# Rotary tables in three parts, a new order of the first lists, and one sum of squares, in a two-layer hybrid encoder

## The chip, the cores and the metric

The kernel runs on one core of one Trainium2 chip. The core has a matrix engine (TensorE, "PE" in the profile; its weight loads appear as "PEld"), a vector engine (VectorE, "DVE"), a scalar engine (ScalarE, "ACT"), a general engine (GpSimd, "POOL"), and a queue engine (SyncE, "SP") that issues the transfers of this kernel. The metric is device time in microseconds (us) for one execution. Each time is one of several runs, of which the median is given.

## The reference, cut to what matters

The input is one sequence of 2048 positions with 1024 features. Two layers are applied, then a final RMS norm. Each layer projects the normed rows to eight sections of 512 columns: query, key, value and gate of an attention with 8 heads of 64, and the same four for a retention with 4 heads of 128.

```python
def rotary_tables(positions, dim):
    inv_freq = 1.0 / (ROPE_BASE ** jnp.linspace(0.0, 1.0, dim // 2, dtype=jnp.float32))
    ang = positions.astype(jnp.float32)[:, None] * inv_freq[None, :]
    return jnp.cos(ang), jnp.sin(ang)

def apply_rotary(t, cos, sin):
    t1, t2 = jnp.split(t, 2, axis=-1)
    ...
    return jnp.concatenate([t1 * c - t2 * s, t1 * s + t2 * c], axis=-1)

def hybrid_layer(x, norm_gain, w_in, w_out, rel_bias, cos, sin):
    hn = rms_norm(x, norm_gain)
    proj = hn @ w_in.astype(hn.dtype)
    aq, ak, av, ag, rq, rk, rv, rg = jnp.split(proj, cuts, axis=-1)
    ya = chunked_rel_attention(aq..., ak..., av..., rel_bias)     # own chunk of 64 + 8 chunks before, softmax
    yr = chunkwise_retention(rq..., rk..., rv..., cos, sin)       # running state per head, rotary phases, group norm
    y = jnp.concatenate([ya * silu(ag), yr * silu(rg)], axis=-1)
    return x + y @ w_out.astype(x.dtype)
```

The kernel needs, for each of the 2048 positions, a table of 64 cosines and one of 64 sines. They are the same for all heads and both layers.

## The kernel before, in words

**Tiling.** The sequence is cut into 16 tiles of 128 rows ("tokens" t = 0 to 15 in the names) and 4 supertiles (n) of 512. The heads are cut into 4 groups (s), each of two attention heads and one retention head. A block is one (layer l, group s, supertile n); there are 32 of them. Single precision is made from pairs of half-precision parts, high and low (`hTh`, `hTl` for the normed and transposed rows, `whT`, `wlT`, `whV`, `wlV` for the weights), with three products for each pair.

**One block.** `dense_T` (line 637) makes the queries and keys in transposed form (tile `dT`, matmuls at line 763). In it, `tab_load` (lines 642 to 647) loads two tables for the supertile, `tabc` (cosine) and `tabs` (sine with its sign), each 128 partitions by 512 columns. The retention's queries and keys are turned in three GpSimd products (lines 703 to 705): the raw rows times `tabc`, the rows with swapped halves (`swp`, two transfers at lines 699 and 700) times `tabs`, and their sum. `dense_V` (line 770) makes values and gates (`dV`, matmuls at line 783). Attention of the block before runs between these matmuls: scores S (lines 831 and 832), bias and maximum on VectorE (line 835), exponent on ScalarE, a scaling on GpSimd (`pq`, line 841), a transpose by a transfer (`pT`, line 843, on SP), and the product with the values (lines 853 and 854).

**The tables.** `tables(ns, wk)` (line 83) computes the angles, the cosine (`k2`), the sine (`r`) and its negative (`ang`) for one or two supertiles in 18 steps. In the work tiles the 128 partitions hold two halves of 64 frequencies: the first 64 partitions for the first 256 positions of the supertile, the other 64 for the second 256. Positions are loaded, spread over 64 partitions, for each half by itself (line 90). `store` (lines 123 to 132) writes the tables to device memory, `tab_d[n]`, with two parts of 128 rows: cosine twice, then negative sine and sine. The supertiles 0; 1 and 2; 3 are computed by three such generators, called in the lists as the steps `t`, `u` and `v`.

**What sets the order.** On TensorE, VectorE, ScalarE and GpSimd the order of instructions is that of the program. In the startup, until the first supertile's `dV` is done, SP's order is that of the program too (`sp_order`, line 1313, left at line 1527). Later a scheduler orders SP's queue, except for transfers marked `in_turn`. The startup's order is written out by hand: one list of step names in `do(...)` (line 1449), in which `x..` steps belong to tokens (`sq` square, `rs` inverse root, `mul` scaling, `tr`, `hi`, `lo` the pair, `dma` the transposes, by transfer, of tokens 4 and up), `W` and `V` steps to weight sections, `g` to gains, `d` to the first block's dense work, `r` to the retention's constants, `bs` and `bt` to the bias. A second list, `listed` (line 1454), gives for each round of the following blocks what is done before and behind the attention step of the round; `run` takes one pair from it per round. Rounds 0 to 11 are `dV` of supertile 0, 12 to 35 the block of supertile 1, 36 to 59 that of supertile 2, 60 to 83 that of supertile 3.

**The output weights.** Before the output projection, `prep_Omax` (line 505) adds up the squares of all output weights of a layer, for one scale: eight slices of 128 columns are loaded (`stO0m`, `stO1m`), squared on ScalarE with the sum of each partition, and added on VectorE slice by slice (lines 520 and 522); then the partitions are summed by a matmul with ones.

Of the kernel before, what the change touches and what calls it, by code (L numbers as in the profile page):

```python
# [10 lines left out]
F32 = mybir.dt.float32  # L11
I32 = mybir.dt.int32
AF = mybir.ActivationFunctionType
ALU = mybir.AluOpType
AX = mybir.AxisListType
# [3 lines left out]
P = 128  # L19
# [8 lines left out]
def hybrid_trunk(ctx: ExitStack, tc: tile.TileContext, x, pos, gain, gcol, w_in, w_out, rel, fgain,  # L28
# [4 lines left out]
    KT = D // P  # L33
    NT = SEQ // P
    NS = SEQ // 512
    NSW = 4
    act, dve, pool, pe, sp = nc.scalar, nc.vector, nc.gpsimd, nc.tensor, nc.sync
# [29 lines left out]

    y_d = [dp.tile([P, D], F32, tag=f"y_d{t}", name=f"y_d{t}") for t in range(NT)]
    x_d = [dp.tile([P, D], F32, tag=f"x_d{t}", name=f"x_d{t}") for t in range(NT)]
    tab_d = [dp.tile([2, P, 512], F32, tag=f"tab{n}", name=f"tab{n}") for n in range(NS)]  # L70


    TWO_PI = 6.283185307179586
# [9 lines left out]
    def tables(ns, wk):  # L83

        ang, k, r, k2 = wk
        pi = k2.bitcast(I32)
        for i, n in enumerate(ns):
            for hf in range(2):
                o = n * 512 + hf * 256
                sp.dma_start(pi[hf * 64:(hf + 1) * 64, i * 256:(i + 1) * 256], pos[None, o:o + 256].to_broadcast([64, 256]))  # L90
        yield

        def mulsub(dst, kk, c):
            dve.scalar_tensor_tensor(out=dst, in0=kk, scalar=-c, in1=dst, op0=ALU.mult, op1=ALU.add)

        def rnd(dst, src, mul):
            dve.tensor_scalar(dst, src, mul, MAGIC, op0=ALU.mult, op1=ALU.add)
            dve.tensor_scalar(dst, dst, -MAGIC, None, op0=ALU.add)  # L98

        act.activation(ang, pi, AF.Copy, scale=invf_sb[:, 0:1])  # L100
        yield
        rnd(k, ang, 1.0 / P1)
        yield
        for c in (PA, PB, PC):
            mulsub(ang, k, c)
            yield
        dve.scalar_tensor_tensor(out=k2, in0=k, scalar=-(PD + PE_), in1=ang, op0=ALU.mult, op1=ALU.add)
        yield
        rnd(k2, k2, 1.0 / TWO_PI)
        yield  # L110
        for kk, c in ((k2, QA), (k, PD), (k2, QB), (k, PE_), (k2, QC)):
            mulsub(ang, kk, c)
            yield
        dve.tensor_scalar(ang, ang, PI_CL, -PI_CL, op0=ALU.min, op1=ALU.max)
        yield
        dve.scalar_tensor_tensor(out=k, in0=ang, scalar=-1.0, in1=ang, op0=ALU.mult, op1=ALU.max)
        yield
        act.activation(r, ang, AF.Sin)
        act.activation(k2, k, AF.Sin, scale=-1.0, bias=quarter[:, 0:1])
        yield  # L120
        act.activation(ang, r, AF.Copy, scale=-1.0)
        yield
        def store(i, n, hf):
            sl = slice(hf * 64, hf * 64 + 64)
            cs = slice(hf * 256, hf * 256 + 256)
            ws = slice(i * 256, i * 256 + 256)
            sp.dma_start(tab_d[n][0, 0:64, cs], k2[sl, ws])
            sp.dma_start(tab_d[n][0, 64:128, cs], k2[sl, ws])
            sp.dma_start(tab_d[n][1, 0:64, cs], ang[sl, ws])
            sp.dma_start(tab_d[n][1, 64:128, cs], r[sl, ws])  # L130
            if hf == 1:
                tab_done.add(n)

        for hf in range(2):
            store(0, ns[0], hf)
            if len(ns) > 1:
                later(7 + 4 * hf, lambda hf=hf: store(1, ns[1], hf))
        yield

    TAB_STEPS = 18  # L140
# [175 lines left out]
    def sumsq(sts, nm, dst):  # L316

        m1 = b2.tile([P, len(sts)], F32, tag="m1", name=f"m1{nm}", bufs=4)
        for i, (st, k0, k1) in enumerate(sts):
            act.activation(st if dst is None else dst[:, k0:k1, :], st, AF.Square, accum_out=m1[:, i:i + 1])  # L320
        if len(sts) == 2:
            dve.tensor_tensor(m1[:, 0:1], m1[:, 0:1], m1[:, 1:2], op=ALU.add)
        return m1[:, 0:1]

    def lowp(m1, nm):
        mb = b2.tile([P, 1], BF16, tag="mb", name=f"mb{nm}", bufs=4)
        dve.tensor_copy(mb, m1)
        return mb
# [175 lines left out]

    def prep_Omax(l, go):
        nm = f"O{l}"
        mm = b2.tile([P, 1], F32, tag="omax", name=f"omax{nm}")
        load = lambda j: load_sec(w_out[l, :, j * P:(j + 1) * P], f"{nm}m{j}")
        for _ in range(4):
            yield  # L510
        sts = [load(0), load(1)]
        for _ in range(4):
            yield
        for j in range(KT):
            yield
            m1 = sumsq(sts[j], f"{nm}m{j}", None)
            if j + 2 < KT:
                sts.append(load(j + 2))
            if j == 0:
                dve.tensor_copy(mm, m1)  # L520
            else:
                dve.tensor_scalar(mm, mm, 1.0, m1[:, 0:1], op0=ALU.mult, op1=ALU.add)
        mm = lowp(mm, nm)
        for _ in range(5):
            yield
        m = allsum(mm, nm)
        sv, iv = norm_scale(m, nm)
        go.os = b2.tile([P, 1], F32, tag="o_s", name=f"o_s{l}")
        go.oi = b2.tile([P, 1], F32, tag="o_i", name=f"o_i{l}")
        dve.tensor_copy(go.os, sv)  # L530
        dve.tensor_copy(go.oi, iv)
        yield
# [73 lines left out]
    def in_turn(i):  # L606

        if not ring.get("free"):
            return
        tc.keep_in_program_order(i)  # L610
# [9 lines left out]
    def later(k, fn):  # L620
        deferred.append([k, fn])
# [15 lines left out]
    def dense_T(l, s, n, g, st):  # L637
        hh, hl = hT[l, n]
        nm = f"{l}_{s}_{n}"
        st.tabc = b1.tile([P, 512], F32, tag="tabc", name=f"tabc{nm}")  # L640
        st.tabs = b1.tile([P, 512], F32, tag="tabs", name=f"tabs{nm}")
        def tab_load():
            while n not in tab_done:
                assert bg
                pull(1)
            in_turn(sp.dma_start(st.tabc, tab_d[n][0]))
            in_turn(sp.dma_start(st.tabs, tab_d[n][1]))

        first = (l, s, n) == (0, 0, 0)

# [794 lines left out]
    def do(names):  # L1445
        for nm in names.split():
            steps[nm]()

    do("xsq0 g g Wsq0 xrs0 Wlp0 xsq1 g Wsc0 t Whi0 xmul0 t xtr0 xrs1 Wlo0 xmul1 xsq2 xhi0 xrs2 Wsq1 xlo0 xtr1 xsq3 "
# [3 lines left out]
    g00.vdone = 4  # L1453
    listed = iter([("bt xrs6 xhi4 xrs5", "xmul6 xlo4 xdma4"), ("xrs7 xmul5", ""), ("xhi5", "xmul7 xlo5"), ("", "xhi6 x8"),
# [16 lines left out]
    att = [None]  # L1471
    for l in range(DEPTH):
        gO = [Grp(), Grp()]
# [142 lines left out]
```

## Time and profile before

| | us |
|---|---|
| three runs | 2039.75, 2034.34, 2036.58 |
| median | 2036.58 |
| the profiled execution | 2034.96 |
| its span in the trace | 2033.0 |
| TensorE busy | 1988.2 (98%) |
| VectorE busy | 1241.9 (61%) |
| ScalarE busy | 1154.5 (57%) |
| GpSimd busy | 705.8 (35%) |

The trace holds the rows of one execution. A row of a timeline gives the start, the duration, the engine, the line of the kernel, the operation, what is written and read, the shape, and in brackets the idle time just before it with what ended it. A group of rows has a count (x256), the busy time, the mean duration, and the idle time before its members. "SPq" is SP's queue: its rows are the issue of a transfer, not the transfer itself; the time from issue to landing stands in the list of transfers. The granted clock is the share of full speed at which TensorE was allowed to run.

### The profile page before, as it was taken

How to read it: one execution, taken by the hardware profiler on the slowest of the kernel's cores; microseconds unless marked ns; L12 is line 12 of the kernel's file. 1: busy time of each engine (PE TensorE's matmuls, PEld its weight loads, DVE VectorE, ACT ScalarE, POOL GpSimd, SP SyncE). 2: the span in 40 equal slices, each digit the busy share in tenths (PEclk: the TensorE clock that was granted, in tenths of full speed). 3: DMA queues.
4: the chain of work that ended last, by engine and by line, in shares of the span. 5: the costliest groups of instructions: out<-in, count | busy, mean ns of one | idle time of the engine just before them, and what ended most of it. 6: DMA issues, size and time to landing. Idle time of an engine off the chain costs nothing.

```text
span 2033.0 us, 36844 instructions
## 1 busy us (share of the span) xinstructions
PE 1988.2 (98%) x12918; PEld 1046.3 (51%) x12918; DVE 1241.9 (61%) x3676; ACT 1154.5 (57%) x2526; POOL 705.8 (35%) x701
## 2 busy tenths in 40 slices
PE   7998999999999999999999999999999999999998
PEld 5444555555555555554444555555555555555544
DVE  7787766665656655676554556565655566557543
ACT  7566756466666655555445556555656565455432
POOL 1444443443344434420003444344434443443100
PEclk9999999999999999999999999999999999999999
DMA  8788775456585754899874547554656665558874
GB/s 232 184 179 163 171 141 128 104 131 140 124 183 123 164 125 104 175 226 268 220 184 101 120 104 164 113 123 104 161 119 146 160 157 133 120 116 188 229 203 135
DMA packets 645690, 313.47 MB, mean 154 GB/s; under 512 B 459232, under 2 KB 602080, under 8 KB 645504
## 3 DMA queue, kind: packets, MB, share of 16 engines
q1 hardware_dynamic: 645504, 311.12, 66.1%
q8 instruction: 101, 1.65, 0.3%
q14 instruction: 85, 0.70, 0.1%
HBM read 123.26 MB, written 41.98 MB: 81 GB/s over the span
## 4 chain that ended last, share of the span: by engine, by line
PE 86%; DMA 4%; DVE 3%; ACT 2%; POOL 2%; issue 2%; SPq 1%; POOLq 0%; ACTq 0%; DVEq 0%
PE dT L763 29%; PE dV L783 27%; PE dO L1161 15%; PE r L888 4%; PE o L853 3%; PE S L832 3%; PE S L831 3%; DMA pT<-pq 2%; PE o L854 2%; POOL swp L704 0%; PE dT L745 0%; DVE sc L835 0%; DMA xa<-in_x_dram 0%; DMA swp<-rot 0%; ACT stO0m L320 0%
## 5 line engine op out<-in xcount | busy, mean ns | idle before, releaser
L841 POOL TENSOR_TENSOR pq<-sc,pq 128x640 f16<-128x640 f32 (+4 forms) x256 | 322.8, 1261 | 958.0 <-ACT pq L840 497.4
L838 ACT ACTIVATE sc<-sc,mq,cT 128x640 f32<-128x640 f32 (+4 forms) x256 | 218.3, 853 | 416.0 <-DVE mq L837 294.2
L783 PE MATMUL dV<-whV,hTh 128*128 128x512 f16 x1024 | 352.1, 380 | 1.1 <-DVE gt L801 1.1
L783 PE MATMUL dV<-wlV,hTh 128*128 128x512 f16 x1024 | 352.2, 380 | 0.0
L783 PE MATMUL dV<-whV,hTl 128*128 128x512 f16 x1024 | 352.0, 379 | 0.0
L763 PE MATMUL dT<-hTh,whT 128*128 128x512 f16 x1008 | 348.3, 381 | 3.1 <-DMA hTh<-hTl 3.1
L763 PE MATMUL dT<-hTh,wlT 128*128 128x512 f16 x1008 | 348.1, 381 | 0.0
L763 PE MATMUL dT<-hTl,whT 128*128 128x512 f16 x1008 | 346.6, 379 | 0.0
L783 PEld LDWEIGHTS <-hTh 128*128 128x128 f16 x2048 | 196.3, 98 | 214.8 <-DVE gt L801 2.6
L763 PEld LDWEIGHTS <-whT 128*128 128x128 f16 x2016 | 192.4, 98 | 209.3 <-DVE xb L98 3.6
L835 DVE CUSTOM_DVE_ANT_0 sc<-S,bias 128x640 f32<-128x640 f32 (+4 forms) x256 | 188.4, 736 | 129.9 <-PE S L832 128.0
L1161 PE MATMUL dO<-whO,yhy 128*128 128x512 f16 x504 | 191.0, 379 | 1.1 <-DMA yhy<-hTh 1.1
L1161 PE MATMUL dO<-whO,yly 128*128 128x512 f16 x504 | 191.0, 379 | 0.3 <-DMA yly<-hTh 0.3
L1161 PE MATMUL dO<-wlO,yhy 128*128 128x512 f16 x504 | 191.0, 379 | 0.0
L840 ACT ACTIVATE pq<-sc 128x640 f16<-128x640 f32 (+4 forms) x256 | 171.5, 670 | 8.1
L1161 PEld LDWEIGHTS <-yhy 128*128 128x128 f16 x1008 | 98.1, 98 | 113.8 <-DMA yhy<-hTh 1.6
L783 PEld LDWEIGHTS <-hTl 128*128 128x128 f16 x1024 | 99.1, 98 | 110.5 <-issue 0.8
L763 PEld LDWEIGHTS <-wlT 128*128 128x128 f16 x1008 | 97.7, 98 | 109.1 <-issue 2.1
L853 PE MATMUL o<-v,pT 128*128 128x129 f16 x1120 | 132.9, 222 | 15.0 <-DMA pT<-pq 15.0
L831 PE MATMUL S<-k,q 128*128 128x128 f16 (+3 forms) x592 | 142.8, 268 | 0.0
L832 PE MATMUL S<-k,q 128*128 128x128 f16 (+3 forms) x592 | 130.0, 268 | 0.0
L853 PEld LDWEIGHTS <-pT 128*128 128x128 f16 x1120 | 103.4, 97 | 50.0 <-DMA pT<-pq 21.5
(360 smaller groups left out, 3295.4 us busy)
## 6 DMA issues: line engine op xcount, KB each, us to landing
q<-qq SPq DMA_DIRECT2D x128, 128.0 KB, 2.4
yyy<-y_d SPq DMA_DIRECT2D x32, 512.0 KB, 4.6
stT<-in_w_in_dram SPq DMA_DIRECT2D x27, 512.0 KB, 4.9
stV<-in_w_in_dram SPq DMA_DIRECT2D x26, 512.0 KB, 4.6
k<-kk SPq DMA_DIRECT2D x128, 64.0 KB, 2.0
swp<-rot SPq DMA_DIRECT2D x64, 128.0 KB, 3.1
tabc<-tab SPq DMA_DIRECT2D x32, 256.0 KB, 3.0
tabs<-tab SPq DMA_DIRECT2D x32, 256.0 KB, 3.1
```

Of the source, the lines that this page charges most:

```text
L763: pe.matmul(ps, w_[:, j, kt, :], h_[:, kt, :], start=(m == 0), stop=(m == 23))
L783: pe.matmul(ps, h_[:, kt, a * P:(a + 1) * P], w_[:, kt, :], start=(m == 0), stop=(m == 23))
L831: pe.matmul(o, st.q[:, hx, 0, cs], k_, start=True, stop=False)
L832: pe.matmul(o, st.q[:, hx, 1, cs], k_, start=False, stop=True)
L835: dve.tensor_tensor_reduce(out=v, in0=S[:, 0:w], in1=g.bias[hx][:, 640 - w:640], scale=1.0, scalar=-3.0e38, op0=ALU.add, op1=ALU.max, accu ...
L838: act.activation(v, v, AF.Exp, bias=m[:, 0:1], scale=g.c[:, 0:1])
L840: act.activation(pq[:, 0:w], v, AF.Copy)
L841: pool.tensor_tensor(pq[:, w:2 * w], v, pq[:, 0:w], op=ALU.subtract)
L853: pe.matmul(o[:, u.hx, 0:129], u.p[:, b, :], v_, start=(b == 0), stop=False)
L854: pe.matmul(o[:, u.hx, 0:65], u.p[:, u.nb + b, :], v_[:, 0:65], start=False, stop=(b == u.nb - 1))
L888: pe.matmul(out_, w_, m_, start=(i == 0), stop=(i + 1 == len(pairs)))
L1161: pe.matmul(ps, h_[:, kt, :], w_[:, kt, :], start=(m == 0), stop=(m == 23))
```

## The change

It has three parts.

1. `tab_d[n]` has three parts of 64 rows (cosine, negative sine, sine) instead of two of 128. Each part is stored by one transfer of both halves (2 × 64 × 256) instead of by one or two transfers for each half, so that three stores take the place of eight for a supertile. The positions of a supertile are loaded by one transfer of two halves instead of two transfers. `tabc` is loaded from the single cosine part, read twice; `tabs` is loaded from the two sine parts, which lie one behind the other.
2. The list of the startup and the list `listed` have the same steps in another order.
3. `prep_Omax` writes the eight sums of squares to eight columns of one tile and adds them up with one reduction at the end.

```diff
-    tab_d = [dp.tile([2, P, 512], F32, tag=f"tab{n}", name=f"tab{n}") for n in range(NS)]
+    tab_d = [dp.tile([3, 64, 512], F32, tag=f"tab{n}", name=f"tab{n}") for n in range(NS)]
...
-            for hf in range(2):
-                o = n * 512 + hf * 256
-                sp.dma_start(pi[hf * 64:(hf + 1) * 64, i * 256:(i + 1) * 256], pos[None, o:o + 256].to_broadcast([64, 256]))
+            src = pos[n * 512:(n + 1) * 512].rearrange("(h c) -> h c", h=2)[:, None, :].to_broadcast([2, 64, 256])
+            sp.dma_start(pi[:, i * 256:(i + 1) * 256], src)
...
-        def store(i, n, hf):
-            sl = slice(hf * 64, hf * 64 + 64)
-            cs = slice(hf * 256, hf * 256 + 256)
-            ws = slice(i * 256, i * 256 + 256)
-            sp.dma_start(tab_d[n][0, 0:64, cs], k2[sl, ws])
-            sp.dma_start(tab_d[n][0, 64:128, cs], k2[sl, ws])
-            sp.dma_start(tab_d[n][1, 0:64, cs], ang[sl, ws])
-            sp.dma_start(tab_d[n][1, 64:128, cs], r[sl, ws])
-            if hf == 1:
-                tab_done.add(n)
-
-        for hf in range(2):
-            store(0, ns[0], hf)
-            if len(ns) > 1:
-                later(7 + 4 * hf, lambda hf=hf: store(1, ns[1], hf))
+        def store(i, n):
+            for part, src in enumerate((k2, ang, r)):
+                sp.dma_start(tab_d[n][part].rearrange("f (h c) -> h f c", h=2), src[:, i * 256:(i + 1) * 256])
+            tab_done.add(n)
+
+        store(0, ns[0])
+        if len(ns) > 1:
+            later(7, lambda: store(1, ns[1]))
...
-            in_turn(sp.dma_start(st.tabc, tab_d[n][0]))
-            in_turn(sp.dma_start(st.tabs, tab_d[n][1]))
+            in_turn(sp.dma_start(st.tabc, tab_d[n][0:1].to_broadcast([2, 64, 512])))
+            in_turn(sp.dma_start(st.tabs, tab_d[n][1:3].rearrange("h f c -> (h f) c")))
...
-        mm = b2.tile([P, 1], F32, tag="omax", name=f"omax{nm}")
+        mm = b2.tile([P, KT], F32, tag="omax", name=f"omax{nm}")
...
-            m1 = sumsq(sts[j], f"{nm}m{j}", None)
+            act.activation(sts[j][0][0], sts[j][0][0], AF.Square, accum_out=mm[:, j:j + 1])
             if j + 2 < KT:
                 sts.append(load(j + 2))
-            if j == 0:
-                dve.tensor_copy(mm, m1)
-            else:
-                dve.tensor_scalar(mm, mm, 1.0, m1[:, 0:1], op0=ALU.mult, op1=ALU.add)
-        mm = lowp(mm, nm)
-        for _ in range(5):
+        yield
+        m1 = b2.tile([P, 1], F32, tag="m1", name=f"m1{nm}", bufs=4)
+        dve.tensor_reduce(m1, mm, axis=AX.X, op=ALU.add)
+        mm = lowp(m1, nm)
+        for _ in range(4):
             yield
...
-    do("xsq0 g g Wsq0 xrs0 Wlp0 xsq1 g Wsc0 t Whi0 xmul0 t xtr0 xrs1 Wlo0 xmul1 xsq2 xhi0 xrs2 Wsq1 xlo0 xtr1 xsq3 "
-       "Wlp1 xmul2 Wsc1 d xhi1 Whi1 xtr2 xrs3 xlo1 xhi2 t Wsq2 xlo2 Wsq3 xmul3 t Wlo1 d d Wlp2 Vsq1 r xtr3 t Vsq0 Wsc2 "
...
+    do("g xsq0 xrs0 Wsq0 xsq1 g Wlp0 g Wsc0 xmul0 Whi0 xtr0 xsq2 t xrs1 xhi0 xmul1 Wsq1 Wlo0 xrs2 t xtr1 xlo0 t Wlp1 "
+       "xmul2 xsq3 xrs3 t d xhi1 Wsc1 t Whi1 xtr2 xlo1 t Wsq2 xmul3 xhi2 Wsq3 xlo2 Wlp2 r d t xtr3 Vsq0 Wlo1 Wsc2 xhi3 "
...
-    listed = iter([("bt xrs6 xhi4 xrs5", "xmul6 xlo4 xdma4"), ("xrs7 xmul5", ""), ("xhi5", "xmul7 xlo5"), ("", "xhi6 x8"),
-                   ("", "xdma5 u xlo6"), ("", "u xhi7"), ("xlo7 bt", ""), ("bt u", "u"), ("", ""), ("u u u", ""),
-                   ("", "xdma6 xdma7"), ("x8 u", "bt"), ("", "u x8"), ("u x8 xin11", ""), ("u", "u u u u"), ("", "u"),
...
+    listed = iter([("xrs5 u xrs6 xmul5 xhi4 bt", "xhi5 xmul6 xlo5"), ("", "xlo4"), ("xdma5", ""), ("bt", "bt xrs7 xhi6"),
+                   ("u u", "xmul7 xlo6"), ("u", ""), ("", ""), ("bt", "xdma4"), ("xhi7 x8 u", "u xdma6"), ("", "xlo7 u"),
+                   ("xdma7", "x8"), ("", "x8"), ("u", "u"), ("xin10 xin9", "u u"), ("u", "x8 u"), ("u u", "u"), ("u", ""),
...
```

32 rows, old and new, of tables (listed, steps) are left out of this document.

## The prediction, made before the changed kernel was run

> **What bounds the kernel now.** I read the busy table, TensorE's waits, the stretches by time, the transfers, and last the timelines where TensorE stood idle. From the page, the busy table, the main queue and one group:
>
> ```profile
> span 2033.0 us, 36844 instructions
> PE 1988.2 (98%) x12918; PEld 1046.3 (51%) x12918; DVE 1241.9 (61%) x3676; ACT 1154.5 (57%) x2526; POOL 705.8 (35%) x701
> q1 hardware_dynamic: 645504, 311.12, 66.1%
> L853 PE MATMUL o<-v,pT 128*128 128x129 f16 x1120 | 132.9, 222 | 15.0 <-DMA pT<-pq 15.0
> ```
>
> TensorE is the bound: busy 1988.2 of 2033.0 us, so 44.8 us are all that can be saved without touching a matmul, and the change only moves a few small ones. What can be lost has no such limit: every transfer that lands after TensorE wants it adds its lateness. `pT`, the transposed softmax weights, does so most. The waits, then the stretches (microseconds, busy time of five engines, granted clock, DMA share, GB/s):
>
> ```profile
> PE o L853 <- DMA pT<-pq: 15.0, 9, 3.1
> PE dT L763 <- DMA hTh<-hTl: 3.1, 1, 3.1
> ```
>
> ```profile
> 20.00:30.00 10.00, 9.59 (x140) 9.09 (x139) 9.37 (x29) 9.59 (x17) 0.55 (x1) 1.00 1.09 332
> ...
> 90.00:125.00 35.00, 31.18 (x184) 15.19 (x182) 29.59 (x71) 21.78 (x52) 19.14 (x19) 0.95 0.77 175
> 150.00:210.00 60.00, 53.13 (x363) 28.16 (x361) 42.94 (x111) 37.46 (x78) 28.14 (x20) 0.97 0.82 172
> 210.00:560.00 350.00, 350.00 (x2380) 187.18 (x2378) 220.27 (x733) 213.45 (x497) 142.25 (x139) 1.00 0.61 133
> 560.00:600.00 40.00, 38.77 (x273) 20.94 (x272) 20.53 (x74) 27.65 (x62) 18.02 (x16) 1.00 0.86 195
> ...
> 69.00:75.50 6.50, 6.50 (x19) 2.42 (x20) 4.76 (x11) 2.67 (x5) 1.38 (x4) 0.54 0.77 259
> 118.80:123.50 4.70, 4.63 (x19) 1.97 (x20) 4.09 (x16) 2.56 (x7) 1.00 (x2) 0.64 1.00 195
> 184.70:189.00 4.30, 4.21 (x25) 2.52 (x26) 1.05 (x3) 0.93 (x2) 0.00 (x0) 0.66 0.58 135
> ```
>
> From 210 to 560 us TensorE never stops. Before 210 it does, in these rows:
>
> ```profile
> 68.99 3.57 PE L763 MATMUL dT<-hTh,whT 128*128 128x512 f16 x8 [3.09 <-DMA hTh<-hTl]
> ...
> 109.72 0.23 PE L853 MATMUL o<-v,pT 128*128 128x129 f16 x1 [1.39 <-DMA pT<-pq]
> ...
> 118.87 0.23 PE L853 MATMUL o<-v,pT 128*128 128x129 f16 x1 [2.43 <-DMA pT<-pq]
> ...
> 168.42 0.23 PE L853 MATMUL o<-v,pT 128*128 128x129 f16 x1 [1.60 <-DMA pT<-pq]
> ...
> 184.79 0.29 PE L853 MATMUL o<-v,pT 128*128 128x129 f16 x1 [3.12 <-DMA pT<-pq]
> ...
> 194.26 0.23 PE L853 MATMUL o<-v,pT 128*128 128x129 f16 x1 [1.63 <-DMA pT<-pq]
> ```
>
> Behind the three longest the granted clock fell: 6.5 us at 0.54 lose 3.0 us, 4.7 at 0.64 lose 1.7, 4.3 at 0.66 lose 1.5. After the waits of 1.6 us or less I saw none such.
>
> **The change part by part.** *Stores and position loads.* SP's queue in the startup:
>
> ```profile
> 42.08 0.55 SPq L127 DMA_DIRECT2D tab<-wk  x1
> ...
> 46.52 0.59 SPq L130 DMA_DIRECT2D tab<-wk  x1
> 47.16 2.51 SPq L90 DMA_DIRECT2D xb<-in_pos_dram  x4
> ...
> 50.99 0.59 SPq L646 DMA_DIRECT2D tabc<-tab  x1
> ...
> 67.00 1.30 SPq L244 DMA_TRANSPOSE hTl<-hTl  x1
> ```
>
> Eight stores take 5.0 us of SP, 0.63 each; five fewer free 3.1 us per supertile. The four position loads take 2.51 us; two fewer free 1.25. Behind both, in one queue in order, stand the tables' loads and the transposes of tokens 4 to 7, the last of which (67.00) TensorE awaits at 68.99. By issue time alone that wait could shrink by 4.4 us, more than its 3.09.
>
> *The shape of the new transfers.* `tabc` was 128 rows; now it is 64 rows read twice, and the first count of its source is 2. The new stores and position loads, two halves of 64 rows, begin with 2 as well. The programmed transfers of before begin with 128, 64 or 16. What old forms took to land:
>
> ```profile
> yyy<-y_d SPq DMA_DIRECT2D x32, 512.0 KB, 4.6
> ...
> tabc<-tab SPq DMA_DIRECT2D x32, 256.0 KB, 3.0
> ...
> y_d<-ya SPq DMA_DIRECT2D x128, 64.0 KB, 1.9
> ...
> pT<-pq SPq DMA_TRANSPOSE x256, 3.0
> ```
>
> No row has a transfer of two halves, so I bound it. Lower end: spread over 16 engines as now, 3.0 us. Upper end: cut only along its first count, it has two engines, each with 128 KB instead of 16. One engine's rate is 332 GB/s / 16 / 1.09 = 19 GB/s in the busiest stretch (20 to 30 us); the fixed part is `y_d`'s 1.9 us less 4 KB at that rate, 1.7. So 1.7 + 6.9 = 8.6 us. By the landing times alone (16 KB more per engine cost 1.6 us from `tabc` to `yyy`, 10 GB/s) it would be 14.5; these hold queueing behind neighbours, so I take the busy stretch's rate. Between 3.0 and 8.6 I take 8.6. By form the nearest row is `tabc`'s own 3.0, but that form starts with a multiple of 16 like all the others and the new one does not. That a transfer is divided along its first count is my assumption, which I hold at 0.78.
>
> The Trainium skill says so too ("DMA: Bandwidth & Descriptors", "Why a DMA increments its semaphore by 16 and not by 1", and "Rules for kernel authors"): the engine count is the largest up to 16 that divides the slowest counts of both patterns, a leading zero-stride broadcast of c copies gets at most c engines, the lowest-numbered. No trace of before shows it. By that rule the sum is the one below; by equal spreading, that of the first rival.
>
> *Who stands behind it.* The tightest and the loosest of the 26 blocks from 305 to 1813 us (leaving out that at 1060), each the issue of `tabc` and the first use of the `pT` that SP issues 1 to 3 us behind it:
>
> ```profile
> 1354.15 0.58 SPq L646 DMA_DIRECT2D tabc<-tab  x1
> ...
> 1361.73 0.22 PE L853 MATMUL o<-v,pT 128*128 128x129 f16 x1
> ...
> 1096.99 0.58 SPq L646 DMA_DIRECT2D tabc<-tab  x1
> ...
> 1107.47 0.22 PE L853 MATMUL o<-v,pT 128*128 128x129 f16 x1
> ```
>
> TensorE uses that `pT` 7.6 to 10.5 us after `tabc`'s issue, 9.05 in the mean of the 26. If two engines first work off `tabc` (8.6) and then 16 KB of `tabs` (0.8), `pT` is whole at about 9.4. Sixteen of the 26 are tighter than that, and their lacks, each 9.4 less its own distance, add up to 14.8 us. At 8.6 the sum is 4.3, at 7.6 nothing, at 10.4 35, at 11 51. I take +14.8. GpSimd's turn reads `tabc` too. In the block in which `tabc` was issued at 357.69 it did so 8.3 us later, after an idle time:
>
> ```profile
> 357.69 0.58 SPq L646 DMA_DIRECT2D tabc<-tab  x1
> ...
> 364.58 1.40 POOL L841 TENSOR_TENSOR pq<-sc,pq 128x640 f16<-128x640 f32 x1 [5.48 <-DMA swp<-rot]
> 365.94 1.27 POOL L703 TENSOR_TENSOR rot<-rot,tabc 128x512 f32<-128x512 f32 x1
> ```
>
> A landing at 8.6 would hold GpSimd 0.3 us there, where it had just been idle 5.48; I cost that at nothing. At 11 us it would hold it 2.7, and the `pq` products queued behind the turn with it, which belongs to the slowest rival.
>
> *First 210 us with narrow transfers.* The first group's three stores put 192 KB on each of two engines: 1.7 + 10.3 = 12.0 us after their start near 43, so landed at 55. `tabc`'s issue waits for that, at 55 instead of 50.99, and everything behind it in SP's queue, the transposes of tokens 4 to 7 first, waits too. The 4.4 us of issue saved lie ahead of that wait and are lost in it. TensorE's wait then ends about 4.5 us later than 68.99: +4.5. For groups 1 to 3 the same stores come in bursts amid the `pT` transposes; the five waits above (10.2 us) stay, and of three bursts of 12 us I let 2 us each reach TensorE: +6, between −5 (their saved issues help) and +15.
>
> *The lists.* The order of steps loses 1.1 us at the start by my hand walk of the lists: the scale of the second weight section is summed after the first dT group, so the first dV starts that much later; this is inside the 4.5, since TensorE waits behind it anyway. With spread transfers it counts by itself. Reordered conversions lie on DVE, which is 85% busy from 90 to 125 us (29.59 of 35), so there it can neither gain nor lose much. Of the moved steps that issue transfers, the four loads of tokens 8 to 11 (`x8`) go from rounds 3 to 13 of the list to rounds 8 to 14, still ahead of their first square, which goes from round 20 to 17; the pairs of transposes of tokens 4 to 7 (`xdma4` to `xdma7`, 1.3 us for one by the row at 67.00) change places on SP; and the inverse root for token 7 (`xrs7`) falls behind a rotary turn on GpSimd, three products of 1.27 us. Each can delay what stands behind it on its queue, a `pT` issue or a token's transposes, by its own length, or hasten it; I cost all of it at 0, ±3.
>
> *Squares.* Per layer eight small DVE additions become one; DVE then no longer waits between ScalarE's squares. The most it can give is the idle time of 560 to 600, 1.2 us, in each of the two layers at best; I take −1.
>
> Sum: 4.5 + 6 + 14.8 + 0 − 1 = +24.3 us. The profiled execution took 2034.96 us and stands 1.6 below the median of 2036.58; from it 2059.3, on the median 2060.9. Forecast: 2060 us.
>
> **The rivals.** *Spread transfers, faster.* If the two-halves form is spread over 16 engines, all lateness above is gone and the saved issues count. The wait at 68.99 falls from 3.09 to about 0.3 and its slow clock (3.0) goes, less the 1.1 of the lists: −4.7. Of the `pT` waits and clocks at 109 to 194 us (10.2 + 1.7 + 1.5 = 13.4) I let 5 go, as DVE limits the rest. With the squares −1: −10.7, 2026 us. For it: `tabc`'s row now; against: its new form. It decides if `tabc` lands within about 4 us.
>
> *Narrow but covered, no change.* If one engine moves 25 GB/s or more, 144 KB and the fixed part take 7.6 us, and no block lacks anything. The startup then loses some 2 us by `tabc`'s later issue: 2038 us. For it: 19 GB/s is measured with all 16 busy; against: the two engines also carry their share of all else, 0.61 busy in 210 to 560.
>
> *Narrow and slower still.* If `pT` is whole only 11 us behind `tabc`, all 26 blocks stall, 51 us, and waits of 3 us bring back the slow clock of the rows above; with 12 in the startup it comes to 2098 us. The 10 GB/s of the landing times speaks for it.
>
> **How the numbers follow.** Chances: forecast 0.45 (own range 2044 to 2080), narrow and slower 0.20, narrow but covered 0.13, spread 0.22. The range runs from 2022, below the spread case by 4, to 2098, the middle of the slowest. A change within 0.3%, 6.1 us, is about what a measurement of this kernel can't tell from none. Faster: the spread case and a little of the covered one, 0.23; same: most of the covered one, 0.10; slower: 0.67.
>
> **What would show it.** `tabc` landing at 7 to 10 us instead of 3.0, and `tab` stores well above 2.1; waits `PE o <- DMA pT<-pq` grown from 15.0 to 30 us or more, with many of about 1 us in the steady blocks, 210 to 560 no longer idle-free; the wait at 68.99 later. If `tabc` lands near 3.0, the first assumption is wrong and with it the sign. If it lands late and `pT` is in time, the sharing of the two engines is milder than I have it.

## The result, and the profile after

| | before | after |
|---|---|---|
| median of five runs, us | 2036.93 | 2123.88 |
| ratio, 95% interval | | 1.0435, 1.0412 to 1.0457 |
| span of the profiled execution | 2033.0 | 2120.0 |
| TensorE busy | 1988.2 | 2013.0 |
| TensorE not busy (span less busy) | 44.8 | 107.0 |

The change makes the kernel 87 us slower. The forecast was 2060 us with a range up to 2098, so the sign was right and the size was missed by a factor of 3.6 (+24 forecast), outside the range. In the trace the 87 us are 62.2 of idle TensorE and 24.8 of longer matmuls. The page of the changed kernel, the lines that answer to those shown of before:

```profile
span 2120.0 us, 36798 instructions
...
PE 2013.0 (95%) x12918; PEld 1052.5 (50%) x12918; DVE 1229.2 (58%) x3662; ACT 1154.0 (54%) x2526; POOL 698.0 (33%) x701
...
q1 hardware_dynamic: 643936, 310.59, 71.3%
...
L844 PE MATMUL o<-v,pT 128*128 128x129 f16 x1120 | 134.8, 223 | 62.5 <-DMA pT<-pq 62.4
```

The queue moved 0.2% fewer bytes than before, yet its packets took 71.3% of the 16 engines' time instead of 66.1%. The wait for `pT` has grown from 15.0 to 62.4 us. TensorE's waits of the changed kernel:

```profile
PE o L844 <- DMA pT<-pq: 62.4, 36, 5.4
PE dV L774 <- DVE gt L792: 9.3, 1, 9.3
PE dT L754 <- DMA hTl<-xa: 5.3, 1, 5.3
PE dV L774 <- ACT raw L686: 4.9, 1, 4.9
```

36 waits instead of 9, with 1.7 us in the mean. Where the time goes along the run can be read from the issues of `tabc`, one in each block, in both traces: the 4th stands 15.2 us later than before (219.57 against 204.37), the 32nd 85.4 later (1898.14 against 1812.73). So the startup and the first blocks cost 15.2 us and the other 28 blocks 70.2, or 2.5 each. Between these two issues, before and after:

```profile
204.37:1812.73 1608.36, 1600.74 (x10543) 844.65 (x10542) 967.32 (x3002) 930.99 (x2089) 589.90 (x576) 1.00 0.64 145
```

```profile
219.57:1898.14 1678.57, 1621.52 (x10545) 849.52 (x10543) 962.44 (x2990) 931.66 (x2090) 589.81 (x576) 0.99 0.70 139
```

Of the 70.2 us, longer matmuls make 20.8 (1621.52 less 1600.74) and idle TensorE 49.4 (57.05 less 7.62). One block, in the timelines of the changed kernel, and behind it the stretch right after the wait:

```profile
594.61 0.55 SPq L637 DMA_DIRECT2D tabc<-tab  x1
...
595.80 4.06 SPq L834 DMA_TRANSPOSE pT<-pq  x1
...
604.77 0.23 PE L844 MATMUL o<-v,pT 128*128 128x129 f16 x1 [3.12 <-DMA pT<-pq]
```

```profile
604.80:609.00 4.20, 4.20 (x26) 2.40 (x27) 1.43 (x5) 1.52 (x2) 2.85 (x3) 0.59 1.20 294
```

`pT` is used 10.2 us behind the issue of `tabc`, after a wait of 3.12 us, and then the granted clock is 0.59 for 4 us. SP itself is held: the issue of this transpose takes 4.06 us. The transpose behind the `tabc` of 357.69 in the trace of before took about half of that (over the 28 blocks of which this can be read, the median is 1.7 us before and 4.1 now):

```profile
358.87 2.18 SPq L843 DMA_TRANSPOSE pT<-pq  x1
```

### The profile page after: what moved, and what is told of

It is laid out like the page before. It is cut to its first block, busy times and chain, and to the rows that moved or that the text cites. A ratio compares the mean times of both kernels' runs of the same rounds, so it can differ in the third digit from the quotient of the medians.

```text
span 2120.0 us, 36798 instructions
## 1 busy us (share of the span) xinstructions
PE 2013.0 (95%) x12918; PEld 1052.5 (50%) x12918; DVE 1229.2 (58%) x3662; ACT 1154.0 (54%) x2526; POOL 698.0 (33%) x701
## 3 DMA queue, kind: packets, MB, share of 16 engines
q1 hardware_dynamic: 643936, 310.59, 71.3%
## 5 line engine op out<-in xcount | busy, mean ns | idle before, releaser
L774 PE MATMUL dV<-whV,hTl 128*128 128x512 f16 x1024 | 360.2, 389 | 0.0
L844 PE MATMUL o<-v,pT 128*128 128x129 f16 x1120 | 134.8, 223 | 62.5 <-DMA pT<-pq 62.4
L822 PE MATMUL S<-k,q 128*128 128x128 f16 (+3 forms) x592 | 145.9, 272 | 0.0
L823 PE MATMUL S<-k,q 128*128 128x128 f16 (+3 forms) x592 | 132.7, 271 | 0.0
```

The costliest lines, as they stand in the source:

```text
L774: pe.matmul(ps, h_[:, kt, a * P:(a + 1) * P], w_[:, kt, :], start=(m == 0), stop=(m == 23))
L822: pe.matmul(o, st.q[:, hx, 0, cs], k_, start=True, stop=False)
L823: pe.matmul(o, st.q[:, hx, 1, cs], k_, start=False, stop=True)
L844: pe.matmul(o[:, u.hx, 0:129], u.p[:, b, :], v_, start=(b == 0), stop=False)
```

## The experiments

All times are medians; each ratio is to the kernel before on the same chip in the same session. The theory: a transfer whose first count is 2 runs on two engines, and `pT`, which needs all of them, comes late behind it. The rivals: the new lists lose; a repeated source is slow in itself; each such transfer has a fixed price; the order in SP's queue is what counts.

**The narrow load by itself, on the kernel before.**

```diff
-            in_turn(sp.dma_start(st.tabc, tab_d[n][0]))
+            in_turn(sp.dma_start(st.tabc, tab_d[n][0:1, 0:64].to_broadcast([2, 64, 512])))
```

> The kernel before with one edit: tabc is loaded as its first 64 rows read twice (source 2 x 64 x 512) instead of 128 rows. Narrow-transfer theory: a load of 256 KB over two engines holds up the pT behind it in every block, so most of the loss of the changed kernel comes back: about +70 us from the 28 blocks behind the startup (the growth from the fourth to the last tabc issue was 15.2 to 85.4 us), 2095 to 2115 us in all. Rival, the new lists or the stores made the loss: within 10 us of 2037.

Measured: 2132.86 us, ratio 1.0464 (1.0428 to 1.0499), more even than the changed kernel and more than expected. The waits of this kernel:

```profile
PE o L853 <- DMA pT<-pq: 75.8, 40, 4.7
```

One line of the change, 32 loads, makes a loss of 93 us. The lists and the stores are those of before, so the loss doesn't need them.

**The narrow load taken out of the changed kernel.**

```diff
-            in_turn(sp.dma_start(st.tabc, tab_d[n][0:1].to_broadcast([2, 64, 512])))
+            for hf in range(2):
+                in_turn(sp.dma_start(st.tabc[hf * 64:hf * 64 + 64, :], tab_d[n][0]))
```

> The changed kernel with one edit: tabc comes in two loads of 64 rows (first count 64) instead of one that reads them twice. Narrow-transfer theory: the steady blocks lose nothing, what is left is the startup with narrow stores and position loads: 2037 + 5 to 15, so 2042 to 2052 us. Rival, lists or stores made the loss in the whole run: above 2100 us.

Measured: 2042.94 us, 1.0020 (1.0007 to 1.0033). The load accounts for 81 of the 87 us (2123.88 less 2042.94). What the other narrow transfers still do is seen below.

**All transfers wide.** As above, and in the same way two stores for each part and two position loads:

```diff
-                sp.dma_start(tab_d[n][part].rearrange("f (h c) -> h f c", h=2), src[:, i * 256:(i + 1) * 256])
+                for hf in range(2):
+                    sp.dma_start(tab_d[n][part][:, hf * 256:hf * 256 + 256], src[hf * 64:hf * 64 + 64, i * 256:(i + 1) * 256])
```

> The changed kernel with every transfer of two halves split into two of 64 rows: six stores for a supertile, two position loads, two tabc loads. Lists, three-part table and the single sum of squares stay. Narrow-transfer theory: this is the first rival of the prediction with two fewer stores saved instead of five: 2026 to 2036 us. Rival, the lists lose in the startup: 2045 us or more.

Measured: 2022.47 us, 0.9929 (0.9903 to 0.9955): 17 us faster than before. This version beats both kernels. Its waits, and the end of its first group:

```profile
PE o L847 <- DMA pT<-pq: 7.7, 9, 2.6
```

```profile
67.95 1.89 PE L757 MATMUL dT<-hTh,whT 128*128 128x512 f16 x8 [0.88 <-DVE hTl L280]
```

The eight matmuls at 67.95 take 1.89 us; the eight at 68.99 of before took 3.57 at the low clock after a wait of 3.09. That is what the prediction's first rival said of this place (wait to 0.3, clock back), at 0.88, but the wide transfers alone don't do it: with the lists of before (last but one experiment) the wait there is 3.38, and in the kernel with the new lists alone it is 2.59.

**The lists alone.** The kernel before with the two new lists.

> The kernel before with the two new lists alone. By the prediction's working (1.1 us later at the first dV, the rest 0 within 3): 2037, from 2034 to 2041 us. Rival, the lists account for the 15 us lost before the fourth block: about 2052 us.

Measured: 2030.70 us, 0.9961 (0.9945 to 0.9977): faster by 9, where I had said no change and the rival said a loss. TensorE's waits for `pT` before 210 us, 10.2 us in five waits before, are now:

```profile
PE o L853 <- DMA pT<-pq: 3.6, 2, 3.4
```

The stretch from 150 to 210 us, which was shown of before, now reads:

```profile
150.00:210.00 60.00, 58.07 (x410) 31.51 (x409) 46.48 (x129) 41.60 (x87) 28.08 (x23) 1.00 0.91 180
```

TensorE is busy 58.07 us instead of 53.13, at full clock, while VectorE does more (46.48 against 42.94). From 90 to 125 us, where I had held VectorE to be the limit, TensorE gains only 0.2 us (31.35 against 31.18).

**Repeated, but 16 engines' worth of first count.**

```diff
-tab_d[n][0:1].to_broadcast([2, 64, 512])
+tab_d[n][0:1, 0:8].to_broadcast([16, 8, 512])
```

> The changed kernel with tabc read as 16 copies of the first 8 rows instead of 2 copies of 64: same bytes, a repeated source as well, but a first count of 16. It leaves out rows 8 to 63 of the cosine table, so the output is another; the work is the same. Theory of few engines: the load is spread again, the steady loss goes, 2042 us as with two loads of 64 rows (2036 to 2046). Rival, reading rows repeatedly is what is slow: at or above 2120 us.

Measured: 2042.65 us, 1.0020 (1.0010 to 1.0030), the same as with two loads of 64 rows. The repeated source costs nothing that can be told; the first count does it.

**Four and eight engines; half and three quarters of the columns.** The same edit with 4 copies of 32 rows, with 8 of 16 (as with 16 copies, the other rows of the cosine table are left out), and (columns) with a narrow load of 256 or 384 columns and two wide loads of the rest:

```diff
+            in_turn(sp.dma_start(st.tabc[:, 0:256], tab_d[n][0:1, :, 0:256].to_broadcast([2, 64, 256])))
+            for hf in range(2):
+                in_turn(sp.dma_start(st.tabc[hf * 64:hf * 64 + 64, 256:512], tab_d[n][0][:, 256:512]))
```

> The changed kernel with tabc read as 4 copies of the first 32 rows (rows 32 to 63 of the cosine table are left out): four engines with 64 KB each. Theory of few engines with the measured lateness (pT in use no sooner than 10 us behind the tabc issue, of which about 8.3 us grow with the bytes of one engine): half of that is saved, pT is there after about 6 us, less than the 7.6 of the tightest block, and the steady loss goes: 2040 to 2052 us. Rival, a fixed price for each transfer with a first count under 16: above 2100 us.

> The changed kernel with half of tabc (256 columns) loaded as two copies of 64 rows, so 64 KB on each of two engines, and the other half in two loads of 64 rows; nothing is left out. Theory of bytes per engine: same lateness as with four engines, and two more issues of 0.6 us for a block: 2042 to 2056 us. Rival, the number of engines itself or a fixed hold of SP's queue decides, whatever the bytes: above 2090 us.

> The changed kernel with tabc read as 8 copies of the first 16 rows (rows 16 to 63 of the cosine table are left out): eight engines with 32 KB each. Point of a curve over the bytes of one engine: 16 KB gave 2043, 64 KB 2061 to 2064, 128 KB 2122 to 2124 us. If the loss is pT's lateness over a slack of at least 7.6 us that grows with the bytes, 32 KB is still covered: 2041 to 2048 us. If each step away from 16 engines costs in proportion: 2054 us.

> The changed kernel with 384 of tabc's 512 columns loaded as two copies of 64 rows (96 KB on each of two engines) and the rest in two loads of 64 rows; nothing is left out. pT should then be there about 8.8 us behind the load, between the 7.7 of 64 KB and the 10 of 128 KB, against slacks of 7.6 to 10.5: the loss lies above half way in bytes but bends, with the slow clock just beginning: 2080 to 2096 us. If the slow clock sets in fully at once: over 2100.

Measured, with the two ends:

| bytes on one engine | form | us | ratio to before | `pT` waits in the trace, us |
|---|---|---|---|---|
| 16 KB | 16 copies of 8 rows | 2042.65 | 1.0020 | 13.0 |
| 32 KB | 8 copies of 16 rows | 2044.25 | 1.0024 | 9.8 |
| 64 KB | 4 copies of 32 rows | 2064.44 | 1.0131 | 22.5 |
| 64 KB | 2 copies of 64 rows, 256 columns | 2060.85 | 1.0109 | 21.0 |
| 96 KB | 2 copies of 64 rows, 384 columns | 2091.93 | 1.0254 | 42.8 |
| 128 KB | 2 copies of 64 rows | 2123.88 | 1.0435 | 62.4 |

Equal bytes on an engine give nearly equal times, on four engines or on two: it is the bytes of one engine, not a fixed price. Up to 32 KB they are covered; from 64 KB on, each 32 KB cost 25 to 34 us (medians, each less its own kernel before), about 1 us for a load. The bend was expected, but both points at 64 KB lie above what I had written (2052 and 2056): the cover ends earlier than at the 7.6 us that I had read as the tightest slack.

**The load behind the `pT`.** In the changed kernel the call of the two table loads comes three rounds later (`later(3, tab_load)` in place of `tab_load()`), so that SP issues them behind that transpose.

> The changed kernel with the tables' loads called three rounds later, so that SP issues them behind the pT transpose that they stood ahead of; shapes unchanged. If the loss is that pT's wait behind the narrow load, most of the steady 70 us goes, though swapped rows and the turn on GpSimd now come later: 2045 to 2085 us. If the narrow load slows everything that runs beside it, wherever it stands: 2110 us or more.

Measured: 2121.90 us, 1.0413 (1.0396 to 1.0431), no gain. What GpSimd waits for in this kernel, and one block of its timelines:

```profile
POOL rot L694 <- DMA tabc<-tab: 166.5, 31, 15.6
```

```profile
439.98 0.55 SPq L637 DMA_DIRECT2D tabc<-tab  x1
...
448.08 1.27 POOL L694 TENSOR_TENSOR rot<-rot,tabc 128x512 f32<-128x512 f32 x1 [4.41 <-DMA tabc<-tab]
```

The later load is no longer hidden from GpSimd: its turn waits 31 times (15.6 us at most), with the `pq` products queued behind it, and the `pT` waits are still 50.7 us. So the experiment doesn't separate what it was made for. But it measures the landing, which no view gives for these loads: 8.1 us from issue to first use here, and between 7.7 and 8.6 in all blocks behind the first two.

**The load on a queue of its own.** `act.dma_start(st.tabc, ...)` in place of `sp.dma_start`: ScalarE issues the narrow load.

> The changed kernel with the narrow tabc load issued by ScalarE instead of SP, so that it no longer stands ahead of pT in SP's queue; the shape, and so the two engines, stay. If pT is late because it stands behind the load in one queue, the steady loss goes: 2045 to 2060 us. If it is late because its own pieces share two engines that are full, it stays: 2090 us or more. In between, engines taking turns between queues: 2060 to 2090.

Measured: 2121.38 us, 1.0403 (1.0389 to 1.0417). A block of its timelines:

```profile
375.56 0.51 ACTq L637 DMA_DIRECT2D tabc<-tab  x1
...
377.75 2.87 SPq L834 DMA_TRANSPOSE pT<-pq  x1
...
385.68 0.23 PE L844 MATMUL o<-v,pT 128*128 128x129 f16 x1 [3.00 <-DMA pT<-pq]
```

`pT` comes from another queue than the load and is again used only 10.1 us behind the load's issue. The order in SP's queue is not what makes it late; the engines that both use are. The trace also keeps a record of each piece (packet) that was moved, with its queue, size, start and duration. Of this `pT`'s 1280 pieces of 256 bytes on SP's queue, 471 start by 379.57 and none until 382.16, and the last at 385.05; the load's 128 pieces, on ScalarE's queue, run until 384.25. (ScalarE also issues the load at another moment than SP did, so the two kernels differ in more than the queue.)

**The position loads, and the tables with the old lists.** The wide version with the narrow position loads put back, and the wide version with the lists of before.

> The version with all transfers wide, but with the narrow position loads (two halves in one transfer) put back. The wide version and the one with narrow stores and position loads stand 20 us apart. If the stores make that, as in the prediction: 2021 to 2026 us. If the position loads do: 2035 to 2043.

> The version with all transfers wide (six stores, two position loads, two tabc loads, three-part table, single sum of squares), with the lists of before. The version with the new lists is 17 us faster than before and the new lists alone 9. If table and squares add to that what is left: 2027 to 2031 us. If the saved issues of SP only help together with the new lists: 2034 to 2040.

Measured: 2023.45 us, 0.9924 (0.9910 to 0.9937), and 2035.49 us, 0.9981 (0.9972 to 0.9990). Narrow position loads cost nothing that can be told. So the 19.5 us between this version and the one with a wide `tabc` alone (2042.94) are the narrow stores'; the stores are the only edit between the two. The longest waits of the one with narrow stores, from 60 to 200 us:

```profile
66.04 0.41 PE L775 MATMUL dV<-whV,hTh 128*128 128x512 f16 x1 [4.18 <-DVE gt L793]
...
96.46 0.29 PE L845 MATMUL o<-v,pT 128*128 128x129 f16 x1 [5.41 <-DMA pT<-pq]
...
191.11 3.57 PE L755 MATMUL dT<-hTl,whT 128*128 128x512 f16 x8 [4.54 <-DMA hTl<-xa]
```

And with the old lists the wide tables and the squares gain 4 us, with the new ones 8 beside the lists' own 9.

**The squares alone.** The kernel before with the new `prep_Omax`.

> The kernel before with the sum of squares in one reduction alone. By the prediction -1 us, at most -2.4, so 2034 to 2037, within what can be told from no change.

Measured: 2037.53 us, 0.9994 (0.9985 to 1.0003), no difference that can be told.

## Why the prediction was right or wrong

**Two engines: right.** The assumption held at 0.78 is what the runs show: with a first count of 16 the loss is gone, with 8 there is none to be told, and with 4 and 2 it grows with the bytes on one engine. The traces show the engines themselves. Of the changed kernel, a stretch in which almost only the load's pieces start and one just behind it, then such a stretch of the kernel with 4 copies; the last two numbers are the share of 16 engines that the pieces begun there took, and GB/s:

```profile
598.50:602.50 4.00, 3.15 (x22) 1.48 (x19) 0.29 (x1) 4.00 (x9) 1.40 (x1) 1.00 0.13 47
603.00:604.00 1.00, 0.00 (x0) 0.00 (x0) 0.00 (x0) 0.00 (x0) 0.00 (x0) 1.00 1.09 259
```

```profile
579.76:581.26 1.50, 1.50 (x9) 0.68 (x8) 0.73 (x3) 1.47 (x3) 0.10 (x1) 1.00 0.26 86
```

0.13 of 16 engines is two, 0.26 is four. The Trainium skill states that a leading repeat of c copies confines a transfer to at most c engines ("DMA: Bandwidth & Descriptors", "Rules for kernel authors"). This case agrees, with 2042.65, 2044.25, 2064.44 and 2123.88 us for 16, 8, 4 and 2 copies. The landing was worked out as 8.6 us and measured at 7.7 to 8.6. That is partly luck: at the 47 GB/s of the first line, 23.5 for an engine and not 19, the 256 KB take 5.6 us, so the fixed part with the share of `tabs` is nearer to 3 us than to the 1.7 that I had. The first two rivals fell: nothing was spread, and nothing was covered.

**"`pT` is whole at about 9.4": the first step that failed.** Where TensorE waited for it in the changed kernel, it could use it only 10.0 to 12.7 us behind `tabc`. Two terms were missing.

The first is the rest of `pT` itself. I let it be whole as soon as the two engines were through with the loads ahead of it. Of the 1280 pieces of the `pT` behind the `tabc` of 594.61, 471 start, then none for 4.7 us, until 602.98, when the two engines are through with the load (8.4 us behind its issue). Only then do the other 809 go, in 1.1 us (the line at 603.00), and TensorE starts 0.7 us behind the last of them. Behind the `tabc` of 357.69 in the trace of before, the 1280 pieces take 1.7 us without a pause. Why the rest of `pT` doesn't go through the other engines meanwhile, no run shows.

The second is a third load. I took the distance from `tabc` to TensorE's use as slack for `tabc` and `tabs` alone. Of the 26 blocks of the prediction, 24 wait in the changed kernel. The 12 in which SP issues nothing between `tabs` and `pT` wait until 10.0 to 10.3 us, whether `pT` was issued 1.2 or 2.2 us behind `tabc`; the five with a load of the bias between until 10.8 to 11.0; and the seven with a load of weights between until 11.2 to 12.7 (in two of the seven, behind the `tabc` of 1365.86 and 1580.58, TensorE starts 1.6 and 2.2 us behind the last piece; why, no run shows). Behind the `tabc` of 489.76 the bias's pieces go two at a time from the end of the load until `pT` resumes. Among the seven are the five blocks with the longest distance. One of them in the trace of before, and the same block in that of the changed kernel:

```profile
305.24 1.16 SPq L646 DMA_DIRECT2D tabc<-tab  x1
...
306.97 0.38 SPq L305 DMA_DIRECT2D stT<-in_w_in_dram  x1
307.46 1.66 SPq L843 DMA_TRANSPOSE pT<-pq  x1
...
315.64 0.22 PE L853 MATMUL o<-v,pT 128*128 128x129 f16 x1
```

```profile
325.93 0.57 SPq L637 DMA_DIRECT2D tabc<-tab  x1
...
327.12 0.59 SPq L297 DMA_DIRECT2D stT<-in_w_in_dram  x1
328.06 4.34 SPq L834 DMA_TRANSPOSE pT<-pq  x1
...
337.12 0.23 PE L844 MATMUL o<-v,pT 128*128 128x129 f16 x1 [0.64 <-DMA pT<-pq]
```

The distance was 10.4 us, by my sum 1 us more than needed, and the block waits all the same, until 11.2. In the 26 blocks of the prediction these waits add up to 42 us, where I had 14.8. The third rival, with `pT` whole at 11 us and 51 us of stalls, came nearer, but its 2098 us was too low as well.

**The slow clock: the term left out of the sum.** I had named it in the slowest rival alone, and without a price there: its 2098 is 2034.96, 51 and 12. Five stretches behind waits, in the changed kernel:

```profile
286.40:290.40 4.00, 4.00 (x33) 2.42 (x34) 1.44 (x5) 2.34 (x5) 2.48 (x2) 1.00 1.04 242
...
714.70:718.70 4.00, 3.93 (x25) 2.68 (x26) 1.44 (x5) 1.34 (x4) 2.62 (x3) 0.57 1.19 286
...
872.97:876.97 4.00, 4.00 (x33) 2.42 (x34) 1.44 (x5) 1.59 (x2) 2.56 (x3) 1.00 1.03 181
...
1216.20:1220.20 4.00, 3.95 (x25) 2.51 (x26) 1.43 (x5) 0.83 (x1) 2.61 (x3) 0.57 0.58 127
1325.00:1329.00 4.00, 3.92 (x25) 2.36 (x26) 1.44 (x5) 1.96 (x6) 2.50 (x2) 0.58 1.18 284
```

They follow waits of 2.26, 2.43, 2.90, 3.35 and 2.29 us. The first and the third kept full clock, the others fell to 0.57 or 0.58 for about 4 us, some 1.7 us lost each. Of the 12 waits of more than 2 us behind the fourth `tabc`, eight were followed by a slow clock and four (2.15, 2.16, 2.26 and 2.90 us) were not; the trace's record of the granted clock accounts for 17 of the 20.8 us by which the matmuls of that stretch are longer. The rest of the 70.2 us is idle time: the waits for `pT` grew there by 45.5 (from 3.6 to 49.1), one wait of 4.9 for ScalarE was added, and about 1 us of other waits fell away.

**The first 210 us: right in kind, too small.** +10.5 was forecast, +15.2 is read at the fourth `tabc`, and that is after the gain of the lists (8.3 at the same place in the kernel with the lists alone). The rows of the changed kernel:

```profile
51.64 1.01 SPq L637 DMA_DIRECT2D tabc<-tab  x1
57.09 0.33 SPq L638 DMA_DIRECT2D tabs<-tab  x1
...
59.35 5.39 SPq L236 DMA_TRANSPOSE hTl<-hTh  x1
...
63.55 1.26 POOL L694 TENSOR_TENSOR rot<-rot,tabc 128x512 f32<-128x512 f32 x1 [15.03 <-DMA tabc<-tab]
...
68.32 1.28 DVE L255 SCALAR_TENSOR_TENSOR hTl<-hTl,rsn,gb 128x1024 f32<-128x1024 f32 x1 [11.37 <-POOL rsn L211]
...
71.69 0.61 PE L774 MATMUL dV<-whV,hTh 128*128 128x512 f16 x1 [9.35 <-DVE gt L792]
```

SP stood until 57.09 for the stores (55 was worked out, for `tabc`; it was `tabs`), then 5.39 us in the issue of one transpose behind the load. But TensorE's wait came on another path than the one I followed, the tokens' transposes. GpSimd's turn stood idle 15.03 us until `tabc` was there, and began at 63.55 instead of 55.10; the inverse root of a token (`rsn`) stood behind that turn on GpSimd; VectorE stood 11.37 us for the root, with `gt` behind it, which TensorE awaited for 9.35. The prediction named an inverse root behind a turn and cost it at nothing, and cost the turn's own wait at nothing from a steady block; in the startup nothing covers either.

**The lists: wrong.** 0 within 3 was forecast (beside the 1.1 of the first `dV`), −9 measured. The step that failed is the cost of the moved steps, put at 0 within 3: with the new lists alone, the `pT` waits before 210 us fall from 10.2 to 3.6. VectorE as the limit held only where I had read it: from 90 to 125 us, 85% busy, TensorE's busy time hardly changed, but from 150 to 210 us VectorE had been busy 72% (42.94 of 60) and there the gain lies. Which of the moved steps makes it, no run shows.

**Squares and position loads: no measurable effect.** −1 was forecast for the squares, and the interval of the run with them alone holds no change.

The steps were taken one behind the other, so they add up by construction: −17 for the version with all transfers wide, +1 position loads, +19.5 stores, +81 `tabc`: +84. The 3 us to the 87 are the difference between the medians of the kernel before in two sessions (2039.83 and 2036.93).

## What to carry to other kernels

Read the first count of both sides of a transfer before counting issues: three stores instead of eight, and one load of two copies, saved SP's time, and the load put 8 times the bytes on each of two engines. Most of the price isn't paid by that transfer but by whatever needs those engines next to it, and it has a threshold: here nothing up to 32 KB on an engine, then about 1 us for each 32 KB and load. When such lateness is summed, count every load that stands ahead of the late transfer on those engines, the rest of the late transfer itself, which here went only behind them, and the slow clock that may follow a wait of 2 us or more.

## What the runs showed of the hardware that I had not expected

A transpose that was under way stood still while two engines worked off a load, and it did so from another queue as well: a queue of its own for the narrow load changed nothing (2121.38 against 2123.88 us). A granted clock of 0.57 to 0.58 came after waits of 2.29 and 2.43 us, while waits of 2.26 and 2.90 us left it at 1.00. The Trainium skill ("TensorE: Matmul & The Clock Gate", "Why this matters for your kernels") puts the limit at gaps of about 3 us; here 2.3 us could be enough and 2.9 us were once not, so the length alone doesn't decide. SP's issue of a transpose next to a narrow load took 4.06 and 5.39 us (2.18 in the block shown of before), so the transfers behind it in SP's queue were issued later too.
